# A ninth output tile by quarters in the first feed-forward's second column half, and eight DRAM sums of the second feed-forward made in its own input stage

## The chip, the cores and the metric

The kernel runs on one core of a Trainium2 chip. A core has a matrix engine (PE, with its weight loads shown as PEld), a vector engine (DVE), ScalarE (ACT), GpSimd (POOL) and SyncE (SP), which here only issues DMAs. The engines run their own lists of instructions in order and wait for each other by semaphores. The metric is the device time of one execution in microseconds (us): the median of three runs of the kernel before is 915.06 us (914.81 to 915.23).

## The reference

One decoder layer over 512 tokens of width 1024, in float32:

```python
x = x + 0.5 * rms_norm(swiglu_ffn(rms_norm(x, norm_pre[l, 0]), ffn1_w_in[l], ffn1_w_out[l]), norm_post[l, 0])
mixed = token_mixer(rms_norm(x, norm_pre[l, 1]), w_mix_in[l], ...)
x = x + rms_norm(mixed, norm_post[l, 1])
x = x + 0.5 * rms_norm(swiglu_ffn(rms_norm(x, norm_pre[l, 2]), ffn2_w_in[l], ffn2_w_out[l]), norm_post[l, 2])
```

`swiglu_ffn` multiplies by `w_in` (1024 x 5632), takes `silu(gate) * up` and multiplies by `w_out` (2816 x 1024). The change concerns this last product of the two feed-forwards, 512 x 2816 by 2816 x 1024.

## The kernel before

**Precision.** Each operand is split into a high part (a cast, on ACT) and a low part (the source less the high part, on DVE), and a product is three matmuls: high x high, high x low, low x high. So each weight tile of 128 x 1024 costs one cast on ACT (line 294) and one subtraction on DVE (line 296), and each tile of activations the same (lines 884 and 885).

**Output stage of a feed-forward** (`ffn_out`). The 2816 hidden rows are 11 tiles of 256 rows, numbered 0 to 10 (`k2`). The output's 1024 columns are two halves of 512. For each half the tiles run in the order that `OUT` gives, and each adds into four PSUM banks `C`. A *plain* tile (`plain`, line 1004) takes 48 matmuls of 128 x 256: 4 chunks of 128 tokens, 2 column quarters, 2 row halves, 3 products of parts. A tile that `QUARTERED` names runs *by quarters* (`quartered` and `product`, line 1012): activations and weights are cut in four blocks, and 7 products of sums of blocks, 6 matmuls each, take the place of 8; four more banks `M` collect four of the products. After the last quartered tile of a half `common` combines these on DVE (ACT copies one), and `add` adds the results into `C` (both line 969 for DVE).

In a half's list the last `LAST` tiles, four in the first feed-forward, do not run tile by tile but chunk by chunk (`chunk`): all four for tokens 0 to 127, then all four for the next 128, so that each chunk can be normalised while the next one runs. In the first chunk the four stand one after the other, later the two column quarters do. `add` for the odd chunks stands ahead of them, `add` for the even ones behind the first chunk.

**Where quarters and sums lie.** Quarters of the activations are made once (`h_quarters`): for tiles 2, 4, 6, 8 in parts of the transposed input (`PLACES`), for tile 3 in two of the three buffers called "raw", for tiles 5, 7 and 9 (`APART`) one part in a "raw" buffer and one in the buffer of the gain row ("gpre"). The sums of blocks (`h_sums`) of a tile that runs by quarters in both halves stay in place of the activations themselves (`stay`); the others go to the buffer "xn". Each half splits the sums again into a three-buffer ring "s" (`s_tile`, `s_place`), in which plain tiles lie too. Tile 7's plain activations of the second half lie where the quarters of 4 and 8 were (`LATER`): the high part in 4's place, the low part in 8's.

**Weights.** `ffn_items` and `mix_items` give the list of weight tiles in the order of their use, `weights` works out after which split each may be loaded. Loads go through two rings of raw buffers ("raw", 3, and "raw2", 5), all issued by SP (line 255); split weights lie in four slots (`WBUF`), and a slot comes free when PE has used its tile. Of a quartered tile's own weights three quarters are split (128 x 768); a second item holds the four sums of its blocks.

**Sums in DRAM.** The sums of weight blocks are made in DRAM (`sums_ahead`): three copies on SP's queue (lines 938 to 940, 512 KB), then three DMAs on POOL's queue that add (line 944), each a step of its own. `make_sums` begins one set and moves all begun ones a step. For the first feed-forward it is called in its input stage (`ffn_in`) at every fifth product from number 15, and in the first half of its output stage. For the second, seven sets are copied at the end of the first feed-forward (`copies_early`) and added in the mixer, six are made in the mixer, and two in the first half of its output stage. `behind(x)` orders an instruction behind `x` on its engine, without a semaphore.

**Input stage** (`ffn_in`): a list of products of 24 matmuls each (line 619). DVE adds raw weight tiles to each other there (line 310).

**Order.** A scheduler that works when the program is built gives each engine its list: the earliest in the program among those that are ready by its own model.

Of the kernel before, what the change touches and what calls it, by code (L numbers as in the profile page):

```python
# [23 lines left out]
PAIRS = NF // 2  # L24
# [60 lines left out]


FIRST = (2, 3, 4, 5, 6, 7, 8, 9)
QUARTERED = {"f1": [FIRST, (2, 3, 4, 6, 8)], "f2": [FIRST, (2, 3, 4, 6, 8, 9, 5)]}
OUT = {"f1": [list(range(PAIRS)), [10, 2, 4, 3, 6, 8, 9, 0, 1, 7, 5]]}
OUT["f2"] = [OUT["f1"][0], [10, 2, 4, 3, 6, 8, 9, 5, 7, 0, 1]]  # L90
LAST, APART, TWICE = {"f1": 4, "f2": 2}, (5, 7, 9), (5, 9)
PLACES, LATER = {2: 1, 4: 2, 6: 0, 8: 3}, {7: (2, 3)}

AGAIN, ROWS = (10,), (18, 19, 20, 21)
EVERY, EARLY, AHEAD = 5, 7, 13

# [25 lines left out]
class Layer:  # L124
# [718 lines left out]
    def ffn_in(self):  # L843

        nc = self.nc
        if not self.second:
            self.begun = ()
            self.sums_due("f1")
        for n, (p, t) in enumerate(ORDER2[len(HEADS2) :] if self.second else ORDER[len(HEADS) :]):
            if n > 14 and n % EVERY == 0 and not self.second:  # L850
                self.make_sums()
            if n == 14 and self.second:

                with self.behind(self.pooled):
                    nc.gpsimd.drain()
            with self.behind(*(self.c22 if p in ("p3", "p5") and self.second else ())):
                self.feed()
            self.c22 = []
            self.lag()
            self.prod(p, t)  # L860
            self.after(p, t)
            if t == PAIRS - 1 and p in ("p3", "p7"):
                self.hs.append(self.h_tile(len(self.hs)))
            if n == 1 and not self.second:
                self.lower_bound()
        self.feed()
        self.lag()
# [96 lines left out]
    def ffn_out(self, gpost_row, scale, after, trans, head):  # L964
# [3 lines left out]
        nc, mm = self.nc, self.nc.tensor.matmul  # L968
        tt = lambda out, a, b, op: nc.vector.tensor_tensor(out, a, b, op=op)
        f = "f2" if self.second else "f1"  # L970
        OF, QF, LF = OUT[f], QUARTERED[f], LAST[f]
        low = self.low
        seq = [(half, k2) for half in range(2) for k2 in OF[half]]
        made = deque((h, None) for h in self.hs)
# [1 line left out]
        kept, again = {}, deque()  # L976

        def more(n):
            while count[0] < min(n, len(seq)):
                half, k2 = seq[count[0]]  # L980
                count[0] += 1
                if k2 in QF[half]:
                    if k2 not in kept or half and k2 in TWICE:
                        stay = k2 in QF[1] and k2 not in TWICE
                        a = self.h_quarters(k2, PLACES.get(k2))
                        with self.behind(*([] if stay else [low])):
                            kept[k2] = a, self.h_sums(k2, stay)
                    a, f = kept[k2]
                    made.append((a, self.s_tile(f)))
                elif half and k2 in AGAIN:  # L990
                    made.append(again.popleft())
                else:
                    made.append((self.h_tile(k2, self.x_place(*LATER[k2]) if half and k2 in LATER else None), None))
                    if not half and k2 in AGAIN:
                        again.append(made[-1])
# [58 lines left out]

        with self.behind(*([self.loaded] if self.second else [])):
            g = self.gain("gpost", gpost_row)
        if self.second:
            self.sums_due("f2", done=AHEAD)
        n = 0
        for half in range(2):  # L1060
            C = [[self.ps() for _ in range(2)] for _ in range(2)]
            M, T, left = None, None, len(QF[half])
            for m, k2 in enumerate(OF[half][: PAIRS - LF * half]):
                more(n + 2)
                h, sums = made.popleft()
                if sums:
                    begin = M is None
                    if begin:
                        M = {p: self.ps() for p in ("p1", "p5", "p7", "p6")}

                    quartered(C, M, h, sums, begin, half and OF[1][m : m + 2] == list(TWICE)[::-1])
                    left -= 1
                    if left == 0:
                        T = common(M, [self.hf[:, j, :] for j in ROWS] if half else [self.st("c") for _ in range(4)])
                else:
                    w = self.pull()
                    more(len(seq) if half and m == PAIRS - LF - 1 else n + 3)
                    for i in (0, 2, 1, 3):
                        for v in range(2):
                            plain(C, w, h, i, v, m == 0)  # L1080
                        if i > 1 and T and m == PAIRS - 1:
                            add(C, T, i % 2)
                    self.drop(w)
                n += 1
                if half == 0 and n % 2:
                    self.make_sums()
                if n == 1:
                    self.prod("p4", PAIRS - 1)
                    self.after("p4", PAIRS - 1)
                self.lag()  # L1090
# [687 lines left out]
    def mixer(self):  # L1778
        nc, tc = self.nc, self.tc
        self.got, self.jobs = set(), deque()  # L1780
        self.sums_due("f2", AHEAD, EARLY)
        with tc.tile_pool(name="ma", bufs=1) as ma:
            self.vh = ma.tile([P, NT, NH, P], F32, name="vh")
            self.qk = ma.tile([P, NT, T], F32, name="qk")
# [193 lines left out]
```

## Time and profile before

| | |
|---|---|
| Median of three runs | 915.06 us |
| The profiled execution | 914.82 us |
| its span, first to last instruction | 913.1 us |
| PE busy | 904.7 us |
| DVE busy | 767.1 us |
| ACT busy | 522.3 us |
| matmuls | 7330 |
| first feed-forward, input stage | about 46 to 223 us |
| its output stage | about 223 to 339 us |
| second feed-forward, input stage | about 626 to 795 us |
| its output stage | about 795 to 907 us |

The profile is of one execution. Each row of a timeline gives start, duration, engine, line, operation, output <- inputs, shapes, a count where equal neighbours were merged, and in brackets the engine's idle time before it with what ended it. Rows of waits give the waiting engine with its tile and line, what it waited for, and us in total, times, longest. A busy time counts an engine's instructions; for PE it is modelled, so spacing from start to start is the better measure of its pace.

### The profile page before, as it was taken

How to read it: one execution, taken by the hardware profiler on the slowest of the kernel's cores; microseconds unless marked ns; L12 is line 12 of the kernel's file. 1: busy time of each engine (PE TensorE's matmuls, PEld its weight loads, DVE VectorE, ACT ScalarE, POOL GpSimd, SP SyncE). 2: the span in 40 equal slices, each digit the busy share in tenths (PEclk: the TensorE clock that was granted, in tenths of full speed). 3: DMA queues.
4: the chain of work that ended last, by engine and by line, in shares of the span. 5: the costliest groups of instructions: out<-in, count | busy, mean ns of one | idle time of the engine just before them, and what ended most of it. 6: DMA issues, size and time to landing. Idle time of an engine off the chain costs nothing.

```text
span 913.1 us, 18148 instructions
## 1 busy us (share of the span) xinstructions
PE 904.7 (99%) x7330; PEld 874.7 (96%) x7330; DVE 767.1 (84%) x1005; ACT 522.3 (57%) x749; POOL 183.2 (20%) x256
## 2 busy tenths in 40 slices
PE   9999999999999999999999999999999999999997
PEld 8999999999999999998888888899999999999997
DVE  6899988889888876699986655699899889988886
ACT  7645545557566557857643345694445545757661
POOL 2541112121111047742230300313000000010002
PEclk9999999999999999999999999999999999999999
DMA  9355779775897825899953127053354445388542
GB/s 311 83 161 140 186 191 213 188 156 137 222 273 237 249 62 143 158 200 210 204 119 116 40 76 253 24 162 95 97 156 140 139 130 156 101 238 242 171 144 93
DMA packets 127921, 146.51 MB, mean 160 GB/s; under 512 B 16335, under 2 KB 100303, under 8 KB 127837
## 3 DMA queue, kind: packets, MB, share of 16 engines
q1 hardware_dynamic: 111868, 130.14, 46.8%
q0 software_dynamic: 15680, 14.69, 11.8%
q8 instruction: 57, 0.93, 0.4%
q10 hardware_dynamic: 288, 0.52, 0.2%
q14 instruction: 28, 0.22, 0.1%
HBM read 143.20 MB, written 31.48 MB: 191 GB/s over the span
## 4 chain that ended last, share of the span: by engine, by line
PE 62%; ACT 0%; DVE 0%; DVEq 0%; POOLq 0%; issue 0%; POOL 0%; ACTq 0%
PE ps L619 23%; PE ps L1012 8%; PE ps L549 6%; PE ps L198 5%; PE ps L200 5%; PE ps L199 5%; PE ps L1004 4%; PE ps L560 1%; PE ps L1441 1%; PE ps L364 1%; PE ps L1540 0%; PE ps L1742 0%; PE ps L1491 0%; PE ps L1715 0%; PE ps L1739 0%; PE ps L1505 0%
## 5 line engine op out<-in xcount | busy, mean ns | idle before, releaser
L294 ACT CAST w<-raw 128x1024 fp32r<-128x1024 f32 x246 | 250.9, 1027 | 190.6 <-PE ps L619 91.7
L296 DVE TENSOR_TENSOR w<-raw,w 128x1024 fp32r<-128x1024 f32 x246 | 299.4, 1221 | 30.7 <-ACT w L294 29.5
L619 PE MATMUL ps<-xq,w 128*128 128x256 f32 x2016 | 236.9, 277 | 0.0
L619 PEld LDWEIGHTS ps<-xq,w 128*128 128x128 f32 x2016 | 232.8, 188 | 0.0
L619 PE MATMUL ps<-sq,w 128*128 128x256 f32 x1512 | 177.6, 276 | 0.0
L619 PEld LDWEIGHTS ps<-sq,w 128*128 128x128 f32 x1512 | 174.2, 188 | 0.0
L310 DVE TENSOR_TENSOR raw<-raw,raw 128x1024 f32<-128x1024 f32 x72 | 89.8, 1252 | 7.1 <-DMA raw<-in_ffn_w_in_dram 5.6
L1012 PE MATMUL ps<-w,hs 128*128 128x256 f32 x672 | 80.9, 276 | 0.0
L1004 PE MATMUL ps<-w,hs 128*128 128x256 f32 x672 | 79.2, 276 | 0.0
L1012 PEld LDWEIGHTS ps<-w,hs 128*128 128x128 f32 x672 | 78.3, 188 | 0.0
L1004 PEld LDWEIGHTS ps<-w,hs 128*128 128x128 f32 x672 | 77.5, 188 | 0.0
L198 PE MATMUL ps<-w,xq 128*128 128x512 f32 x176 | 71.1, 404 | 0.0
L200 PE MATMUL ps<-w,xq 128*128 128x512 f32 x176 | 68.9, 392 | 0.0
L199 PE MATMUL ps<-w,xq 128*128 128x512 f32 x176 | 68.6, 390 | 0.0
L944 POOL DMA_DIRECT2D f2sums<-in_ffn_w_out_dram x15 | 20.2, 1522 | 178.6 <-DMA f2sums<-in_ffn_w_out_dram 178.1
L549 PE MATMUL ps<-xq,w 128*128 128x256 f32 x480 | 55.7, 278 | 0.0
L549 PEld LDWEIGHTS ps<-xq,w 128*128 128x128 f32 x480 | 54.9, 188 | 0.5 <-issue 0.5
L884 ACT CAST hs<-hf 128x1024 fp32r<-128x1024 f32 x32 | 33.7, 1053 | 27.4 <-PE ps L1012 19.7
L885 DVE TENSOR_TENSOR hs<-hf,hs 128x1024 fp32r<-128x1024 f32 x32 | 39.1, 1223 | 9.0 <-ACT hs L884 8.4
L944 POOL DMA_DIRECT2D f1sums<-f1sums x26 | 22.0, 847 | 108.6 <-DMA f1sums<-in_ffn_w_out_dram 57.4
L944 POOL DMA_DIRECT2D f2sums<-f2sums x30 | 26.3, 911 | 85.7 <-DMA f2sums<-in_ffn_w_out_dram 44.6
L310 POOL TENSOR_TENSOR raw<-raw,raw 128x1024 f32<-128x1024 f32 x12 | 32.6, 2722 | 40.9 <-DVE w L296 40.7
(263 smaller groups left out, 1234.2 us busy)
## 6 DMA issues: line engine op xcount, KB each, us to landing
raw<-in_ffn_w_in_dram SPq DMA_DIRECT2D x98, 512.0 KB, 4.7
raw<-in_ffn_w_out_dram SPq DMA_DIRECT2D x44, 512.0 KB, 5.5
raw<-in_w_mix_in_dram SPq DMA_DIRECT2D x28, 512.0 KB, 4.7
raw<-f2sums SPq DMA_DIRECT2D x15, 512.0 KB, 5.1
raw<-f1sums SPq DMA_DIRECT2D x13, 512.0 KB, 6.4
raw<-in_w_mix_out_dram SPq DMA_DIRECT2D x8, 512.0 KB, 4.3
f2sums<-in_ffn_w_out_dram SPq DMA_DIRECT2D x30, 128.0 KB, 4.9
f2sums<-in_ffn_w_out_dram SPq DMA_DIRECT2D x15, 256.0 KB, 6.4
```

Source lines behind the costliest of these rows:

```text
L198: mm(ps, sh, mh, start=start, stop=False, **kw)
L199: mm(ps, sh, ml, start=False, stop=False, **kw)
L200: mm(ps, sl, mh, start=False, stop=stop, **kw)
L294: nc.scalar.copy(hi, raw)
L296: self.low = nc.vector.tensor_tensor(lo, raw, hi.bitcast(F32), op=ALU.subtract)
L310: added = (nc.vector if late else nc.gpsimd).tensor_tensor(o, o, c, op=ALU.add)
L549: mm(ps[:, u0:u1], w[:, a, k, :], self.xop(k, b, u0, u1), start=k + n + m == 0, stop=k == ND - 1 and n == 2, skip_group_check=True,)
L619: self.nc.tensor.matmul(ps[:, c], wb[b][:, k, v], left[d][:, k, :], start=first and a + n + k == 0, stop=n == 2 and k == KH - 1, skip_grou ...
L885: self.nc.vector.tensor_tensor(lo, src, hi.bitcast(F32), op=ALU.subtract)
L944: nc.gpsimd.dma_start(to[:, a:b], v, accum_op=ALU.add)
L1004: mm(out, a[kk][:, i * P : (i + 1) * P], w[:, b, kk, QUARTER * v : QUARTER * (v + 1)], start=begin and c == kk == n == 0, stop=kk == 1 and ...
L1012: mm(ps[:, QUARTER * c : QUARTER * (c + 1)], A[a][:, c], B[b], start=begin and c == n == 0, stop=n == 2, skip_group_check=True,)
```

## The change

Tile 9 runs by quarters in the second half of the first feed-forward too, where it was plain, and stands second in the order (10, 9, 2, 4, 3, 6, 8, then 0, 1, 7, 5) where it stood seventh. Its sums and quarters are those of the first half, kept in the "xn", "raw" and gain buffers. `TWICE` becomes a list for each feed-forward, empty for the first. The sums of the first feed-forward are 14 sets instead of 13, and the calls of `make_sums` in the input stages begin at product 10. The second feed-forward makes eight sets (all but the seven early ones) in its own input stage; the mixer only finishes the early ones.

```diff
-QUARTERED = {"f1": [FIRST, (2, 3, 4, 6, 8)], "f2": [FIRST, (2, 3, 4, 6, 8, 9, 5)]}
-OUT = {"f1": [list(range(PAIRS)), [10, 2, 4, 3, 6, 8, 9, 0, 1, 7, 5]]}
+QUARTERED = {"f1": [FIRST, (2, 3, 4, 6, 8, 9)], "f2": [FIRST, (2, 3, 4, 6, 8, 9, 5)]}
+OUT = {"f1": [list(range(PAIRS)), [10, 9, 2, 4, 3, 6, 8, 0, 1, 7, 5]]}
-LAST, APART, TWICE = {"f1": 4, "f2": 2}, (5, 7, 9), (5, 9)
+LAST, APART, TWICE = {"f1": 4, "f2": 2}, (5, 7, 9), {"f1": (), "f2": (5, 9)}
...
-EVERY, EARLY, AHEAD = 5, 7, 13
+EVERY, EARLY = 5, 7
...
-            self.sums_due("f1")
+        self.sums_due(*(("f2", None, EARLY) if self.second else ("f1",)))
...
-            if n > 14 and n % EVERY == 0 and not self.second:
+            if n > 9 and n % EVERY == 0:
                 self.make_sums()
...
-        OF, QF, LF = OUT[f], QUARTERED[f], LAST[f]
+        OF, QF, LF, two = OUT[f], QUARTERED[f], LAST[f], TWICE[f]
...
-                    if k2 not in kept or half and k2 in TWICE:
-                        stay = k2 in QF[1] and k2 not in TWICE
+                    if k2 not in kept or half and k2 in two:
+                        stay = k2 in QF[1] and k2 not in APART
...
-        if self.second:
-            self.sums_due("f2", done=AHEAD)
...
-                    quartered(C, M, h, sums, begin, half and OF[1][m : m + 2] == list(TWICE)[::-1])
+                    quartered(C, M, h, sums, begin, half and OF[1][m : m + 2] == list(two)[::-1])
...
-        self.sums_due("f2", AHEAD, EARLY)
+        self.sums_due("f2", EARLY, EARLY)
```

## The prediction

> **What bounds the kernel now.** I read the page's head first, then the waits of the matrix engine (PE) alone, then the chain of work that ended last, in order of time.
>
> ```profile
> span 913.1 us, 18148 instructions
> PE 904.7 (99%) x7330; PEld 874.7 (96%) x7330; DVE 767.1 (84%) x1005; ACT 522.3 (57%) x749; POOL 183.2 (20%) x256
> PE ps L194 <- POOL ones L172: 1.2, 1, 1.2
> PE ps L364 <- DVE xn L754: 0.5, 1, 0.5
> PE ps L619 <- ACT xq L384: 0.2, 1, 0.2
> 595.65 199.00 PE ps L619 x1752
> 794.65 5.44 PE ps L1004 x48
> 808.25 38.08 PE ps L1012 x336
> ```
>
> PE waits for others 1.9 us in all, three times, by the three rows of its waits. In the chain its matmuls follow each other without a gap: 48 plain ones (L1004) take 5.44 us, 336 of the quartered kind (L1012) 38.08 us, which is 113.3 ns each in both, and 1752 of the input stage (L619) 199.00 us, 113.6 ns each. So the time is the number of matmuls, and nothing that is taken from the vector engine (DVE), from ScalarE (ACT) or from a DMA can be gained. Only two things move the end: fewer matmuls, or a new wait of PE.
>
> **The ninth tile by quarters.** A plain output tile is 48 matmuls (4 token chunks, 2 column quarters, 2 row halves, 3 products of high and low parts), a quartered one 42 (7 products of 2 x 3). Six go: 6 x 113.3 ns = **-0.68 us**, all on the path. The Trainium skill ("TensorE: Matmul & The Clock Gate", section "Wait — 56ns, not 53.3ns?") gives the spacing of warm matmuls as columns over 2.4 GHz plus some 2.5 ns; for 256 columns that is an estimate of 109 ns, and the six would be worth 0.66 us by it. The rows say 113.3 ns and decide.
>
> For the six matmuls the change adds one more set of sums of tile 9: three copies on SP's queue, three adding DMAs on POOL's, one more load of 512 KB, one more split of 1024 columns, while the split of tile 9's own weights shrinks from 1024 to 768. The activations cost no new DVE work: quarters and sums of tile 9 exist since the first half, and their second split stands where the plain tile's split stood. Beside five quartered tiles of the same kind, all without a PE wait, I cost these at nothing. The hiding is the 4.76 us that PE needs for a tile.
>
> **Buffers held longer.** Tile 9's quarters lie in a "raw" buffer and in the gain buffer, and stay there now until its second use. Before, both came free with its first use:
>
> ```profile
> 275.12 0.42 SPq L255 DMA_DIRECT2D raw<-in_w_mix_in_dram  x1
> 275.59 2.67 SPq L165 DMA_DIRECT2D gpre<-in_norm_pre_dram  x1
> 300.08 1.29 SPq L255 DMA_DIRECT2D raw<-in_w_mix_in_dram  x2
> 326.48 1.43 DVE L481 SCALAR_TENSOR_TENSOR xn<-xs,col,gpre 128x512 f32<-128x512 f32 x2 [2.06 <-POOL col L458]
> ```
>
> The first mixer weight and the gain row are loaded at 275. As tile 9 is now the second of the half, they can be issued one plain and one quartered tile later, about 290, and the two loads at 300 (tile 3's buffers) one tile later, about 305. The gain row is read first at 326, so some 30 us of cover are left. Cost nothing. SP loses 2.67 us to the gain row at the new place instead of the old one; loads behind it have the five-buffer ring as cover.
>
> **The end of the half.** Here the change takes a cushion away. Before, the order was 8 (quartered), 9 (plain), then the last four tiles 0, 1, 7, 5 chunk by chunk. Under the 5.44 us of plain tile 9, DVE combined the products of the quarters (L969), split the last activations (L885) and the last weights (L296). Now tile 8 is directly followed by the four.
>
> ```profile
> 306.12 2.88 PE L1012 MATMUL ps<-w,hs 128*128 128x256 f32 x24
> 308.85 0.84 PE L1012 MATMUL ps<-w,xq 128*128 128x256 f32 x6
> 309.52 8.32 PE L1004 MATMUL ps<-w,hs 128*128 128x256 f32 x72
> 308.09 1.23 DVE L296 TENSOR_TENSOR w<-raw,w 128x1024 fp32r<-128x1024 f32 x1 [0.35 <-ACT w L294]
> 309.23 0.68 DVE L969 TENSOR_TENSOR hf<-ps,hf 128x512 f32<-128x512 f32 x1
> 309.83 1.22 DVE L885 TENSOR_TENSOR xq<-hf,xq 128x1024 fp32r<-128x1024 f32 x1
> 310.96 0.69 DVE L969 TENSOR_TENSOR hf<-ps,hf 128x512 f32<-128x512 f32 x1
> 311.56 1.22 DVE L296 TENSOR_TENSOR w<-raw,w 128x1024 fp32r<-128x1024 f32 x1
> 312.69 0.68 DVE L969 TENSOR_TENSOR hf<-hf,ps 128x512 f32<-128x512 f32 x1
> 313.29 1.22 DVE L885 TENSOR_TENSOR hs<-hf,hs 128x1024 fp32r<-128x1024 f32 x1
> 314.43 0.69 DVE L969 TENSOR_TENSOR hf<-ps,hf 128x512 f32<-128x512 f32 x1
> 315.03 1.29 DVE L969 TENSOR_TENSOR ps<-ps,hf 128x512 f32<-128x512 f32 x2
> 316.25 1.23 DVE L885 TENSOR_TENSOR hs<-hf,hs 128x1024 fp32r<-128x1024 f32 x1
> 317.40 1.22 DVE L296 TENSOR_TENSOR w<-raw,w 128x1024 fp32r<-128x1024 f32 x1
> 309.05 1.06 ACT L884 CAST hs<-hf 128x1024 fp32r<-128x1024 f32 x1 [0.99 <-PE ps L1012]
> ```
>
> Tile 8 ends on PE at 309.52; plain tile 9 would end at 314.96. DVE is busy without a hole from 308.09 to 318.6: weights (tile 1's next in the ring), then the four combining steps with the splits between them, the two additions, and last the activations and weights of tile 5. Start to start a split takes 1.14 us and a combining step or an addition 0.61.
>
> After the change tile 8 ends one quartered tile later, 309.52 + 4.76 = 314.28, and the four tiles begin at once, 12 matmuls or 1.36 us each in the first chunk: 0 at 314.28, 1 at 315.64, 7 at 317.00, 5 at 318.36; the second chunk at 319.72. What needs tile 8's end cannot move forward: the low part of tile 7 (it overwrites tile 8's quarters), the activations of tile 5 (buffer of tile 8's sums; ACT began that kind of cast at 309.05, so 313.81 now), the weights of tile 5 (slot of tile 8's sums), and the combining. Tile 1's activations are done before, one tile's distance earlier than in these rows.
>
> DVE's list by the order of the rows, shifted by 4.76: weights of 7 from 312.85, combining 1 to 314.60, low part of 7 to 315.73, combining 2 to 316.34, weights of 5 to 317.48, combining 3 to 318.09, activations of 5 to 319.23, combining 4 to 319.84, addition for column quarter 0 to 320.45. PE wants tile 7's low part at 317.2 (there is cover of 1.5 us), tile 5's weights at 318.47 (1 us), tile 5's low activations, its third matmul, at 318.59: it gets them at about 319.3, **0.7 us late**. The first chunk then ends at 320.4 and the addition comes 0.1 us late. Sum: +0.76 us. If DVE takes the third and fourth combining step behind everything PE waits for, the lateness is 0.1; if it takes both before tile 5's activations and starts with combining instead of weights, 1.6. I take 0.76, because the rows show one split between each two combining steps, and keep both ends. Queued behind the late split are the fourth step and the additions; the next chunk and the output of chunk 0 wait for them, nothing else does.
>
> **The eight sums of the second feed-forward.** Six leave the mixer and two leave the output stage; all eight go to the input stage, calls at products 10 to 60. PE waits nowhere in the mixer, so nothing is won there. What they meet is this:
>
> ```profile
> DMA to landing us min/median/max: 3.7/5.6/9.8
> DMA to landing us min/median/max: 3.5/3.6/4.6
> DVE raw L310 <- DMA raw<-in_ffn_w_in_dram: 5.6, 3, 2.1
> 664.78 25.48 SPq L255 DMA_DIRECT2D raw<-in_ffn_w_in_dram  x8
> 679.63 1.23 DVE L310 TENSOR_TENSOR raw<-raw,raw 128x1024 f32<-128x1024 f32 x1 [1.54 <-DMA raw<-in_ffn_w_in_dram]
> 686.25 1.22 DVE L296 TENSOR_TENSOR w<-raw,w 128x1024 fp32r<-128x1024 f32 x1
> 804.09 1.25 POOL L944 DMA_DIRECT2D f2sums<-in_ffn_w_out_dram  x1 [174.79 <-DMA f2sums<-in_ffn_w_out_dram]
> 128.90 0.60 SPq L940 DMA_DIRECT2D f1sums<-in_ffn_w_out_dram  x1
> ```
>
> The first two rows are the "raw" tile's in two windows: loads land after 5.6 us (median) in the first feed-forward's input stage, 60 to 185 us, where sums are made, and after 3.6 in the second's, 640 to 785, where none are. In the second, DVE waits for a load three times already, 2.1 us at most. POOL's queue is free there (idle 175 us up to 804). The Trainium skill ("DMA: Bandwidth & Descriptors", section "Issuing engines are not separate DMA queues") says that DMAs of all issuers run on the same 16 engines and interleave; the two medians agree, and it is the rule that speaks against this part.
>
> The worst place is 679.63. The second and third sum are both ordered behind the last load of tile 4, so six copies of 0.60 us of SP time each stand ahead of tile 5's loads. PE's product 24 of this stage begins, 38 products of 2.73 us before 794.65, at 691.0 and reads low parts 0.9 us later; DVE had that split done at 686.25 + 1.22 = 687.5: 4.4 us of cover. With the median of the first stage a load is 2.0 us later, and PE sees nothing. With its longest (9.8 against 4.6) it is 5.2 later, and PE stands 0.8 us. I cost it at 0.
>
> The first feed-forward's calls begin at product 10 instead of 15, but both calls are ordered behind the same load (the last of tile 4), so the 14 sums end where the 13 did. Nothing.
>
> **Sum.** 914.82 us (the profiled execution's own time; 1.7 us lie around its span) - 0.68 + 0.76 = 914.9. The median of the runs shown is 0.24 above that execution, so 915.1 for the measured one: the change gives back at the end of the half what it saves in it.
>
> **Rivals.** *The six matmuls stay saved* (0.30): DVE does the splits first, wait 0.1, 914.5 on the median. For it: the same slots, and an order that is set ahead of time could put the split first. Against it: in the rows the combining steps never wait for a split that is ready beside them by more than one. *Late weight loads in the second input stage* (0.12): the same mechanism at all the tiles' bursts, each over the cover by 0.8 us or, where two sums stand ahead of one burst, by 2. It decides when a load lands more than 4.4 us later than now. Two such places and the forecast's wait give 915.1 + 1.5 to 4, about 917: slower. Against it: with sums in the first stage DVE has no DMA among its waits at all. *The order of DVE or SP elsewhere changes* (0.06), by up to 2 us either way. The forecast itself has 0.52; between 0.1 and 1.6 us of wait it is 914.5 to 916.0.
>
> **Chances.** A measurement of this kernel can tell about 0.2% (1.8 us) from no change, so all cases but the late loads are "the same": same 0.86, slower 0.10 (most of the late loads, some of the reordering), faster 0.04 (reordering alone, since six matmuls are a third of what counts). The range goes from the saved case less 0.4 of scatter (914.1) to the lower late loads (916.5).
>
> **What would show it.** L1012 has 42 more matmuls and L1004 48 fewer. Tile 8's last matmul comes directly before the four tiles. PE's waits gain one row with L1004 and DVE as releaser, or a gap in L1004's spacing some 4 us after tile 8, of 0.7 us; no gap there means the first rival. Loads of the second input stage land at 5 to 6 us in the median, and DVE's wait for them grows above 5.6 us; a PE wait at L619 means the second. A change of more than 2 us with none of these would make my reading wrong altogether.

## The result and the profile after

| | before | after |
|---|---|---|
| median of the timed runs | 914.93 us (914.67 to 915.23, 4 runs) | 926.44 us (924.40 to 928.48, 4 runs) |
| ratio, 95% interval | | 1.0127 (1.0106 to 1.0148) |
| profiled execution, its own time | 914.82 us | 928.48 us |
| its span | 913.1 us | 926.6 us |

The changed kernel is slower by 11.5 us, far above the predicted range. One run of a kernel further down took 1531 us at a granted clock of 0.56 where its others took 915 to 922, and is left out of its median. Of the prediction's rivals one came about, the late weight loads in the second input stage, at two to six times its price: 8.7 us by the run of that part alone, where it was given 1.5 to 4. The head of the page after, two of its groups of instructions and its row of weight loads (its last figure is the median from issue to landing, 4.7 before):

```profile
span 926.6 us, 18156 instructions
PE 908.3 (98%) x7324; PEld 877.2 (95%) x7324; DVE 765.3 (83%) x1006; ACT 522.6 (56%) x750; POOL 187.6 (20%) x259
L310 DVE TENSOR_TENSOR raw<-raw,raw 128x1024 f32<-128x1024 f32 x72 | 89.7, 1250 | 20.0 <-DMA raw<-in_ffn_w_in_dram 18.6
L1004 PE MATMUL ps<-w,hs 128*128 128x256 f32 x624 | 74.0, 277 | 0.3 <-DVE hs L885 0.3
raw<-in_ffn_w_in_dram SPq DMA_DIRECT2D x98, 512.0 KB, 5.1
```

PE has its six matmuls fewer (x7324 against x7330), and L1004 has 48 fewer (672 before). But DVE stood 18.6 us at L310, the addition of two raw weight tiles, until a weight load had landed; before it was 5.6 us. Of the waits of PE alone, after, those that bear on the change (total, times, longest, in us):

```profile
PE ps L619 <- DVE ps L638: 7.1, 3, 4.7
PE ps L619 <- DVE w L296: 1.6, 1, 1.6
PE ps L560 <- ACT w L294: 0.7, 1, 0.7
PE ps L1004 <- DVE hs L885: 0.3, 1, 0.3
```

The first two rows are new: 8.7 us at L619 in the second input stage, most of it for L638, of which the prediction said nothing. The timeline of the place, first PE, then DVE (start, duration, then in brackets the idle time ahead and what ended it):

```profile
687.03 1.98 PE L619 MATMUL ps<-xq,w 128*128 128x256 f32 x16
690.56 3.91 PE L619 MATMUL ps<-xq,w 128*128 128x256 f32 x32 [1.55 <-DVE w L296]
699.13 4.58 PE L619 MATMUL ps<-sq,w 128*128 128x256 f32 x24 [4.66 <-DVE ps L638]
...
678.96 0.68 DVE L638 TENSOR_TENSOR hf<-ps,hf 128x512 f32<-128x512 f32 x1
688.14 1.23 DVE L310 TENSOR_TENSOR raw<-raw,raw 128x1024 f32<-128x1024 f32 x1 [8.50 <-DMA raw<-in_ffn_w_in_dram]
...
698.29 0.69 DVE L638 TENSOR_TENSOR ps<-ps,hf 128x512 f32<-128x512 f32 x1
```

And the same two instructions before, from its timeline, for tile 4 and for tile 6:

```profile
689.78 0.69 DVE L638 TENSOR_TENSOR ps<-ps,hf 128x512 f32<-128x512 f32 x1
738.55 0.69 DVE L638 TENSOR_TENSOR ps<-ps,hf 128x512 f32<-128x512 f32 x1
...
691.02 2.88 PE L619 MATMUL ps<-sq,w 128*128 128x256 f32 x24
740.04 2.88 PE L619 MATMUL ps<-sq,w 128*128 128x256 f32 x24
```

L638 at 689.78 is the subtraction that the function `after` issues for product p5 of tile 4: the bank of p5 less a copy, written into the bank on which product p6 then adds. It ended at 690.47, and p6 began at 691.02: 0.55 us of cover, the time by which it can be late before PE waits. For tile 6 it is 740.04 - 739.24 = 0.80. DVE works its list in order, so whatever makes DVE late, a load ahead of an addition too, makes this subtraction late. After, DVE stood 8.50 us for the load, was busy without a hole from then on (before, it was busy for 132.9 of the 145 us from 640 to 785, or 92%, which leaves little to catch up with), and p6 began at 699.13. The wait of 1.55 us ahead of it is that for the late load's own data: before, their low part was split at 682.0, and PE, whose third set of eight matmuls in a product reads it, wanted it at 685.58 + 1.82 = 687.4, so they had 5.4 us of cover.

The same row shows the second price: 24 matmuls took 4.58 us instead of 2.88. The windows, after first and then before (the numbers are busy us and instructions of PE, PEld, DVE, ACT, POOL, then the granted clock of PE, the DMA share and GB/s):

```profile
699.40:702.80 3.40, 3.40 (x18) 3.40 (x17) 3.37 (x5) 0.64 (x2) 0.85 (x1) 0.50 0.90 188
752.00:786.00 34.00, 34.00 (x289) 34.00 (x290) 29.60 (x32) 15.89 (x20) 4.51 (x5) 1.00 0.79 197
```

```profile
699.40:702.80 3.40, 3.40 (x32) 3.40 (x31) 3.31 (x4) 1.71 (x3) 0.00 (x0) 1.00 0.46 148
752.00:786.00 34.00, 34.00 (x302) 34.00 (x302) 31.88 (x39) 19.37 (x27) 0.00 (x0) 1.00 0.47 140
```

Behind the wait of 4.66 us the granted clock was 0.50 for 3.41 us, which costs half of it, 1.7 us. And in the 34 us from 752, behind a wait of 1.99 us at tile 6's p6, PE ran 289 matmuls instead of 302 at a granted clock of 1.00: 13 x 0.1133 = 1.5 us, of which more below. At the end of the first feed-forward the trace loses 0.44 us in the first chunk and 0.66 us more than before at the mixer's first product, and wins 0.68. So of the 13.66 us between the two profiled executions, 8.7 are the waits, 1.7 the half clock, 1.5 the slower matmuls, 0.4 the end of the first feed-forward; 0.3 lie in the start of the kernel (the first L619 at 11.40 instead of 11.07), where the change does nothing, and some 1.1 us I do not place.

### The profile page after: what moved, and what is told of

It is laid out like the page before. It is cut to its first block, busy times and chain, and to the rows that moved or that the text cites. A ratio compares the mean times of both kernels' runs of the same rounds, so it can differ in the third digit from the quotient of the medians.

```text
span 926.6 us, 18156 instructions
## 1 busy us (share of the span) xinstructions
PE 908.3 (98%) x7324; PEld 877.2 (95%) x7324; DVE 765.3 (83%) x1006; ACT 522.6 (56%) x750; POOL 187.6 (20%) x259
## 4 chain that ended last, share of the span: by engine, by line
PE 50%; DVE 5%; DMA 3%; issue 3%; POOL 1%; ACT 1%; DVEq 0%; POOLq 0%; ACTq 0%
PE ps L619 12%; PE ps L1012 8%; PE ps L549 6%; PE ps L198 5%; PE ps L200 5%; PE ps L199 5%; PE ps L1004 4%; DMA raw<-in_ffn_w_in_dram 3%; DVE w L296 3%; DVE raw L310 1%; PE ps L560 1%; PE ps L1439 1%; POOL raw L310 1%; PE ps L364 1%; DVE ps L638 1%
## 5 line engine op out<-in xcount | busy, mean ns | idle before, releaser
L294 ACT CAST w<-raw 128x1024 fp32r<-128x1024 f32 (+1 forms) x247 | 251.4, 1026 | 201.2 <-PE ps L619 79.6
L296 DVE TENSOR_TENSOR w<-raw,w 128x1024 fp32r<-128x1024 f32 (+1 forms) x247 | 300.2, 1219 | 32.3 <-ACT w L294 30.9
L619 PE MATMUL ps<-xq,w 128*128 128x256 f32 x2016 | 237.6, 277 | 1.6 <-DVE w L296 1.6
L619 PEld LDWEIGHTS ps<-xq,w 128*128 128x128 f32 x2016 | 233.3, 188 | 1.8 <-DVE w L296 1.8
L619 PE MATMUL ps<-sq,w 128*128 128x256 f32 x1512 | 180.2, 278 | 7.1 <-DVE ps L638 7.1
L619 PEld LDWEIGHTS ps<-sq,w 128*128 128x128 f32 x1512 | 176.5, 189 | 7.6 <-issue 7.0
L310 DVE TENSOR_TENSOR raw<-raw,raw 128x1024 f32<-128x1024 f32 x72 | 89.7, 1250 | 20.0 <-DMA raw<-in_ffn_w_in_dram 18.6
L1012 PE MATMUL ps<-w,hs 128*128 128x256 f32 x696 | 83.7, 276 | 0.0
L1012 PEld LDWEIGHTS ps<-w,hs 128*128 128x128 f32 x696 | 81.1, 188 | 0.0
L1004 PE MATMUL ps<-w,hs 128*128 128x256 f32 x624 | 74.0, 277 | 0.3 <-DVE hs L885 0.3
L1004 PEld LDWEIGHTS ps<-w,hs 128*128 128x128 f32 x624 | 72.1, 188 | 0.5 <-DVE hs L885 0.5
L944 POOL DMA_DIRECT2D f1sums<-f1sums x28 | 24.0, 857 | 117.3 <-DMA f1sums<-in_ffn_w_out_dram 55.8
L310 POOL TENSOR_TENSOR raw<-raw,raw 128x1024 f32<-128x1024 f32 x12 | 32.6, 2723 | 40.9 <-DVE w L296 40.7
L200 PEld LDWEIGHTS ps<-w,xq 128*128 128x128 f32 x176 | 33.0, 188 | 7.5 <-DVE xq L371 0.3
```

The source lines that it names most:

```text
L200: mm(ps, sl, mh, start=False, stop=stop, **kw)
L294: nc.scalar.copy(hi, raw)
L296: self.low = nc.vector.tensor_tensor(lo, raw, hi.bitcast(F32), op=ALU.subtract)
L310: added = (nc.vector if late else nc.gpsimd).tensor_tensor(o, o, c, op=ALU.add)
L619: self.nc.tensor.matmul(ps[:, c], wb[b][:, k, v], left[d][:, k, :], start=first and a + n + k == 0, stop=n == 2 and k == KH - 1, skip_grou ...
L944: nc.gpsimd.dma_start(to[:, a:b], v, accum_op=ALU.add)
```

## The experiments

The theory after the result, A: the copies of the moved sums stand ahead of the weight loads in SP's queue and share the DMA engines with them; the loads land late, DVE waits, and PE waits for L638. The rivals are in the expectations, where the letters B and C can stand for other things from run to run. Each run is compared with runs of the kernel before on the same chip (medians 914.74 to 915.16 us).

**The two parts apart.** The first part alone: of the change, the edits to the second feed-forward's sums are undone.

```diff
...
-        self.sums_due(*(("f2", None, EARLY) if self.second else ("f1",)))
+        if not self.second:
+            self.sums_due("f1")
...
-            if n > 9 and n % EVERY == 0:
+            if n > 9 and n % EVERY == 0 and not self.second:
...
+        if self.second:
+            self.sums_due("f2", done=AHEAD)
...
-        self.sums_due("f2", EARLY, EARLY)
+        self.sums_due("f2", AHEAD, EARLY)
```

> The first feed-forward's part alone; the second feed-forward makes its sums where the kernel before does (six in the mixer, two in the output stage). Theory A (the loss is the DRAM copies that stand ahead of weight loads in the second input stage): about 915.4 us, that is -0.68 for six matmuls, +0.43 for the wait at tile 5's activations and some +0.6 where the mixer's first product waits for the late chain of the chunks, and no wait of PE after 345 us. Rival C (the first part shifts the order of everything behind it): several us above 915, with waits in the second input stage.

The second part alone is the change without its edits to QUARTERED, OUT, TWICE and the places that read them; the calls for the first feed-forward's sums begin at product 15, as before.

> The eight sums of the second feed-forward in its input stage, on the kernel before. Theory A: about 924 to 927 us, with the same waits of PE for DVE near product 22 to 24 (together above 5 us). Rival C: about 915.

The first part alone: 916.99 us (915.80 to 922.58, 10 runs), 1.0033 (1.0015 to 1.0051), no PE wait in the second input stage. The second alone: 923.62 us (921.95 to 924.67, 4 runs), 1.0093 (1.0076 to 1.0110), and the waits of the change:

```profile
PE ps L619 <- DVE ps L638: 5.1, 2, 4.7
```

So the second part is most of the loss, some 8.7 of 11.5 us; rival C, that the first part shifts everything behind it, falls. The first part costs 2.0 us, more than predicted and more than the 915.4 us expected for it here, and its runs scatter by 7 us; that is taken up at the end.

**One set at a time.** The two sets that are begun at one call (the prediction's worst place) are spread.

```diff
-                self.make_sums()
+                self.make_sums(not (self.second and n == 20))
...
-    def make_sums(self):
+    def make_sums(self, begin=True):
...
-        if n < 2 and self.ahead:
+        if begin and n < 2 and self.ahead:
```

> The whole change, but the call at product 20 of the second input stage begins no set, so that one set of copies, not two, stands behind the last load of tile 4, and each later set comes one call later. Theory A (two sets of copies, 1 MB in SP's queue ahead of tile 5's loads): the load that landed after 11.9 us lands in 5 to 7, the waits of 1.6 and 4.7 us go with the throttled stretch behind them, and the time is 917 to 919. Rival B (any traffic of the sums in this stage, POOL's adding DMAs above all): above 922 us, with the waits only moved.

924.09 us (918.76 to 927.62, 5 runs), 1.0090 (1.0060 to 1.0121): theory A is missed, and it is what rival B forecast, above 922 with the waits only moved. The wait at tile 4 is gone, but one has come up at tile 6 (timeline of PE):

```profile
744.90 5.46 PE L619 MATMUL ps<-sq,w 128*128 128x256 f32 x24 [3.44 <-DVE ps L638]
```

Tile 6's p6 has 0.80 us of cover before. Single sets make loads late enough to use that up; the pair was not the point.

**Copies and adding DMAs apart.** One kernel issues the copies of the eight sets in the mixer and leaves the adding DMAs where the change has them.

```diff
...
-            self.making.append(self.sums_ahead(*self.ahead.popleft()))
+            g = self.sums_ahead(*self.ahead.popleft())
+            if self.park:
+                next(g)
+                self.parked.append(g)
+            else:
+                self.making.append(g)
+        elif not self.park and self.parked:
+            self.making.append(self.parked.popleft())
...
```

> The whole change, but the three copies of each of the eight sets are issued in the mixer; only POOL's adding DMAs stay in the second input stage. Theory A: no wait of PE there, 915.0 to 916.5 us. Rival B (POOL's adding DMAs delay the loads): above 920 us.

940.88 us (938.25 to 943.51, 4 runs), and it tells something else. As nothing held them in the second input stage, the adding DMAs were issued in the mixer too, in POOL's queue ahead of POOL's selects (`affine_select`), for which DVE waits and then PE:

```profile
PE ps L1680 <- DVE pT L1642: 20.9, 1, 20.9
```

The second input stage, without any DMA of the sums, had no PE wait in this run. Two more kernels separate them, both on the second part alone: one leaves out the 24 adding DMAs, and with them the additions of these sums; one has the copies in the mixer and each adding DMA held in the stage by a one-column copy on POOL.

```diff
...
-                nc.gpsimd.dma_start(to[:, a:b], v, accum_op=ALU.add)
+                f == "f2" and self.second or nc.gpsimd.dma_start(to[:, a:b], v, accum_op=ALU.add)
...
```

> The second part of the change alone, with the 24 adding DMAs of its eight sets left out (the second half's sums of the second feed-forward are then copies, not sums); the 24 copies on SP's queue stay where they are. Theory A (the copies stand ahead of the weight loads in SP's queue and share the DMA engines with them): loads land late as with the adds, PE waits for DVE's subtraction (L638) at some product p6 by 2 us or more, 919 to 924 us. Rival B (the adding DMAs of POOL's queue slow the loads): no PE wait in the stage, 915 to 916. Rival C (it is the sum of both kinds of traffic; either alone stays nearly under the cover): loads late by 1 to 3 us, PE waits under 1 us, 915 to 917.

```diff
...
-            with self.behind(*([self.selected] if f == "f2" else [])):
+            seen = [nc.gpsimd.tensor_copy(self.col(), self.half(self.whole[0], 0)[:, 0, :1])] if self.second else []
+            with self.behind(*([self.selected] if f == "f2" else []), *seen):
...
```

> The counterpart: the copies of the eight sets are issued in the mixer, and only their 24 adding DMAs stay in the second input stage, each behind a one-column copy on POOL that reads an activation of the tile finished last, so that none can be issued in the mixer. Theory A: no PE wait in the stage, 915 to 916. Rival B: PE waits at L638 by 2 us or more, 919 to 924. Rival C: as for the copies alone, 915 to 917.

Copies alone: 918.10 us (917.36 to 918.14, 5 runs), 1.0034 (1.0022 to 1.0047). Adding DMAs alone: 917.21 us (915.56 to 923.52, 10 runs), 1.0039 (1.0022 to 1.0056). The first row of PE's waits in each, copies first:

```profile
PE ps L619 <- DVE ps L638: 1.6, 1, 1.6
```

```profile
PE ps L619 <- DVE ps L638: 3.5, 2, 3.1
```

By the medians neither A nor B: the rival that it is the sum of both is nearest, though both lie above its 915 to 917. Each kind of traffic alone costs about 2.5 to 3.4 us, both together 8.7. By the medians that is more than the sum; by the intervals (2.0 to 4.3, 2.0 to 5.1 and 7.0 to 10.1 us) the sum is not excluded. The profiled executions say this with two limits. That of the copies took 918.10, as the median, but of its 3.2 us over the kernel before only 2.6 arise in this stage; 1.1 lie in a stretch of slower matmuls from 47 us on, ahead of any of these copies. That of the adding DMAs took 923.52, the slowest of the ten runs: by its wait of 3.1 us and the half clock behind it rival B's sign is there in this run, but the median run cannot have lost as much. The weight loads of the stage, issue to landing, as far as the traces tell their landing (8 to 20 of some 34), in us: 3.5/3.6/4.6 before (least, median, most), 3.4/4.6/8.4 with the copies, 3.6/5.3/8.9 with the adding DMAs, and after the change

```profile
DMA to landing us min/median/max: 3.6/4.9/11.8
```

For the load that DVE stood for in the changed kernel, two rows of SP tell whether it was issued late or landed late, after first and then the same load before:

```profile
676.20 0.37 SPq L255 DMA_DIRECT2D raw<-in_ffn_w_in_dram  x1
```

```profile
674.65 0.37 SPq L255 DMA_DIRECT2D raw<-in_ffn_w_in_dram  x1
```

PE was 1.45 us behind the kernel before at that place (687.03 against 685.58), so the load was issued 0.1 us late; it is the one of 11.8 us and landed about 7 us late. So SP's time for issuing the six copies is not what made this load late; it lost its time between issue and landing. That adding DMAs suffice for late loads, with no copy ahead in SP's queue, the run with them alone shows. How much the copies add by standing ahead in the queue and how much by using the same DMA engines is not told apart.

**The cover itself.** In the kernel before, without any sums in the stage, DVE's subtraction for p5 is done four times for tile 4 (cover 0.55 us) and for tile 7 (5.99 us), with PE's order pinned.

```diff
...
-            tt(self.two_by(q), self.two_by(bank["p5", t]), h1, ALU.subtract)
+            [tt(self.two_by(q), self.two_by(bank["p5", t]), h1, ALU.subtract) for _ in range(4 if self.second and t in (4, 7) else 1)]
```

> The kernel before, with no sums in the second input stage, but DVE's subtraction between the products p5 and p6 done four times instead of once (same operands, same result) for tile 4 and for tile 7 of that stage, and PE's order pinned to that of before. Three more at 0.61 us from start to start are 1.8 us. Theory: the cover of a late DVE is the one at p6: 0.55 us for tile 4, 5.99 for tile 7. PE waits 1.3 us for L638 at tile 4's p6, not at all at tile 7's, and the time is 916.1 to 916.5. Rival (the prediction's cover, 4.4 us by the low parts of the weights): no PE wait at all, 914.8 to 915.2.

919.10 us (916.63 to 920.53, 5 runs), 1.0045 (1.0032 to 1.0058). In the timelines, tile 4 first, then tile 7 (L620 is L619 there):

```profile
692.25 2.62 DVE L638 TENSOR_TENSOR ps<-ps,hf 128x512 f32<-128x512 f32 x4
695.02 4.26 PE L620 MATMUL ps<-sq,w 128*128 128x256 f32 x24 [3.10 <-ACT ps L653]
...
757.91 0.70 DVE L638 TENSOR_TENSOR ps<-ps,hf 128x512 f32<-128x512 f32 x1
759.35 2.88 PE L620 MATMUL ps<-sq,w 128*128 128x256 f32 x24
```

Tile 4's last repeat ends at 694.87, and PE starts 0.15 us behind it, the distance it has behind L638 in the changed kernel too; the row names ACT's L653, which ended in the same moment, but p6 does not need that: before, it began at 692.24, when p6 was under way. The subtraction is done 4.4 us later than before (690.47), 3.7 if one takes off that PE itself was 0.7 us behind there. That is more than the 1.8 I gave it, because a weight split and another subtraction were placed between the repeats. PE waits 3.10 us, about the 3.7 less 0.55 of cover. At tile 7 the last repeat ends at 758.61, 11.0 us later than the one subtraction before (747.64), of which 5.7 are PE's own shift (759.35 against 753.64); of 5.99 us of cover 0.74 are left, and PE does not wait. The theory holds in place and kind; the size was off, and behind the 3.10 us stands a half clock of 3.41 us that I had not reckoned with. Wait and half clock, 3.10 + 1.7 us, are most of the 5.7 that this profiled execution, the slowest of the five, lost.

**More cover for tile 4.** On the second part alone, product p2 of tile 4 goes ahead of p6.

```diff
+for _t in (4,):
+    _n = ORDER2.index(("p6", _t))
+    ORDER2[_n : _n + 2] = ORDER2[_n + 1], ORDER2[_n]
```

> The second part of the change alone (the eight sums in the second input stage, as in the run of that part, 923.62 us), with one edit: of tile 4, product p2 goes ahead of p6, so that DVE's subtraction between p5 and p6 has one product, 2.72 us, more of cover there (0.55 + 2.72 = 3.3 us). Theory: the loads land as late as in that run, but PE's wait for L638 at tile 4's p6 falls from 4.7 to about 2, under the 3.1 us behind which the clock was halved, so that the half clock (6.83 us at half, 3.4 us) goes too: 923.6 - 2.7 - 3.4 = 917.5, within 916 to 919.5. Rival (the late loads themselves are the bound, through the weights that are split from them): PE waits as long for the weights (L296) instead, 922 or more.

921.92 us (920.75 to 923.20, 4 runs), 1.0073 (1.0060 to 1.0086): only 1.7 us better, outside the 916 to 919.5 expected.

```profile
695.66 2.98 PE L619 MATMUL ps<-sq,w 128*128 128x256 f32 x24 [1.66 <-DVE ps L638]
...
746.43 4.60 PE L619 MATMUL ps<-sq,w 128*128 128x256 f32 x24 [3.28 <-DVE ps L638]
```

At tile 4 the wait fell to 1.66 us and the half clock behind it went, as the theory had it; PE did not wait longer for weights, so the rival falls. But now tile 6, whose cover was left at 0.8, waited 3.28 us with a half clock behind it. With several thin places and loads late by chance, one place mended is not the stage mended.

**The first part: the cushion.** Two ways to put 5.44 us of plain matmuls back between tile 8 and the chunks: three tiles by chunks instead of four, or plain tile 10 moved there.

```diff
-LAST, APART, TWICE = {"f1": 4, "f2": 2}, (5, 7, 9), {"f1": (), "f2": (5, 9)}
+LAST, APART, TWICE = {"f1": 3, "f2": 2}, (5, 7, 9), {"f1": (), "f2": (5, 9)}
```

> The first part of the change alone, with the last three tiles of the first feed-forward chunk by chunk instead of the last four, so that tile 0 stands as a plain tile (48 matmuls, 5.44 us) between the quartered tile 8 and the chunks, as tile 9 did before. If the missing 5.44 us of plain matmuls are what cost 0.44 us in the first chunk and 0.66 at the mixer's start, both gaps go and the six matmuls are won: 914.2 to 914.6. Rival (the chunks, now of 18 matmuls per column quarter instead of 24, are too short for DVE's work between them): new PE waits in the chunks, 915.5 or more.

```diff
...
-OUT = {"f1": [list(range(PAIRS)), [10, 9, 2, 4, 3, 6, 8, 0, 1, 7, 5]]}
+OUT = {"f1": [list(range(PAIRS)), [9, 2, 4, 3, 6, 8, 10, 0, 1, 7, 5]]}
...
-AGAIN, ROWS = (10,), (18, 19, 20, 21)
+AGAIN, ROWS = {"f1": (), "f2": (10,)}, (18, 19, 20, 21)
...
```

> The first part of the change alone, with plain tile 10 moved from the front of the second half to the place between the quartered tile 8 and the last four (order 9, 2, 4, 3, 6, 8, 10, then 0, 1, 7, 5), so that 5.44 us of plain matmuls lie there as tile 9's did before; its activations are split a second time for it (before, the split of the first half was used again), and a bank is opened by the first product into it. If the missing cushion is what the first part costs: no PE wait for L886 in the first chunk and the mixer's start as before, 914.96 - 0.68 = 914.3, within 914.0 to 914.9. Rival (something else of the ninth quartered tile costs it): 916 to 917 as with the first part alone.

Three tiles: 920.13 us (918.71 to 923.25, 5 runs), 1.0054 (1.0041 to 1.0068); the rival. PE waits for the normalised rows of the chunks, which the shorter chunks do not cover:

```profile
PE ps L364 <- DVE xn L481: 1.5, 2, 1.2
...
PE ps L364 <- DVE hf L481: 1.1, 1, 1.1
```

These are 2.6 us of the 8.4 that this profiled execution, at 923.25 the slowest of the five, is behind the kernel before. In the mixer PE waits 1.7 us more (L1442), and matmuls ran slower at full clock in stretches between 346 and 419 us; the loss is not fully taken apart.

Tile 10 moved: the waits at the chunks are gone (one of 0.4 us for L491 comes up at the front of the half), but the median is 918.37 us, 1.0038 (1.0022 to 1.0054), with runs from 915.19 to 922.16. Two further profiles of it were to show where the long runs lose their time.

> The kernel of the run with tile 10 ahead of the last four, once more: its twelve times lay between 915.19 and 922.16 us, while the profiled one (916.42) had no PE wait in the second input stage. Theory: the longer ones have the same stall as the eight sums bring, PE waiting for DVE's subtraction (L638) ahead of a product p6 with 0.2 to 0.8 us of cover, because one weight load landed late by chance. If this profile is one above 918 us, it shows such a wait and, where the wait is above 3 us, the half clock. Rival: the time is lost at many places or at the start, with no wait above 1 us.

> As the run before it, for a second profile of the same kernel: theory and rival as there.

The first took 914.87 us, the second 920.49 us, beside 915.16 for the kernel before. Neither waited in the second input stage; the theory falls. The long one stood in the mixer (waits of PE, then timelines of POOL and DVE):

```profile
PE ps L1677 <- DVE pT L1639: 4.1, 1, 4.1
...
486.17 0.81 POOL L945 DMA_DIRECT2D f2sums<-f2sums  x1 [2.73 <-DMA f2sums<-f2sums]
486.76 1.50 POOL L1629 TENSOR_SCALAR_AFFINE_SELECT e<-e 128x512 f32<-128x512 f32 x2
487.72 1.29 DVE L1639 SCALAR_TENSOR_TENSOR pT<-ps,e 128x512 f32<-128x512 f32 x2 [9.80 <-POOL e L1629]
```

The same instructions in the kernel before:

```profile
472.56 0.81 POOL L944 DMA_DIRECT2D f2sums<-f2sums  x1 [2.82 <-DMA f2sums<-f2sums]
473.16 1.51 POOL L1624 TENSOR_SCALAR_AFFINE_SELECT e<-e 128x512 f32<-128x512 f32 x2
...
481.89 1.28 DVE L1634 SCALAR_TENSOR_TENSOR pT<-ps,e 128x512 f32<-128x512 f32 x2
```

POOL issues the adding DMAs of the mixer one behind the other, each behind the landing of what it reads, and the selects stand behind the last. Before, the last issue of that chain began at 472.56 and the first pair of selects ended at 474.67, 7 us ahead of DVE's need. In the first part alone the last issue began at 479.65, and in this run at 486.17. The last two runs take one of the 13 sets out of the mixer (the output stage makes it), with the orders of PE, DVE and ACT unchanged:

```diff
-EVERY, EARLY, AHEAD = 5, 7, 13
+EVERY, EARLY, AHEAD = 5, 7, 12
```

> The first part alone with tile 10 moved ahead of the last four, and one set of the second feed-forward's sums made in the output stage instead of the mixer (12 sets there instead of 13); orders of PE, DVE and ACT are the same as without. Theory (POOL's chain of adding DMAs in the mixer made the scatter): the selects come some 9 us sooner, about 474, DVE does not wait for them over 1 us, no run above 917, median 914.5 to 915.0. Rival (the scatter has another source): runs up to 922 again, median above 916.5. Rival 2 (the set is now late in the output stage, where the DMA engines are over 90% busy): PE waits there, 915.5 or more.

> The first part as the change has it (tile 8 directly ahead of the last four), with 12 sets in the mixer instead of 13. Theory: without the scatter of the mixer what is left is the lost cushion: -0.68 for the six matmuls, +0.44 in the first chunk, +0.66 - 0.24 at the mixer's start, so 914.96 + 0.2 = 915.2, within 914.9 to 915.9, no run above 917.5. Rival: 916.5 and above as before, with long runs.

With tile 10 moved: 915.84 us (914.67 to 917.93, 11 runs), 1.0013 (1.0004 to 1.0022). As the change has it: 916.14 us (915.39 to 917.29, 11 runs), 1.0014 (1.0005 to 1.0024). The long runs are gone, and in the profile of the first the selects begin long before DVE needs them, and DVE waits for PE alone:

```profile
464.42 0.65 POOL L1629 TENSOR_SCALAR_AFFINE_SELECT e<-e 128x512 f32<-128x512 f32 x1 [2.85 <-ACT e L1628]
479.35 1.29 DVE L1639 SCALAR_TENSOR_TENSOR pT<-ps,e 128x512 f32<-128x512 f32 x2 [0.32 <-PE ps L1637]
```

So POOL's chain made the scatter, by one long run that was profiled and by the two kernels in which a shorter chain took it away; why the chain runs later in the kernels with the first part than before is not shown. Both medians are above what I expected, by about 1 us, and one run, 917.93, is above the 917 set for the first; no version tried beats the kernel before. The first part costs 2.0 us as the change has it and about 1.3 without the scatter, not the 0.1 that was predicted. The two gaps and the six matmuls explain 0.4 of it; putting the cushion back by tile 10 took the gaps away and gained only 0.3, within the intervals, so the rest is open.

## Why the prediction was wrong

*Six matmuls, -0.68.* Right: x7324, with 48 of L1004 gone.

*The end of the half, +0.76 for tile 5's activations.* Right in place and kind, less in size, and incomplete. The wait in the chunk and the mixer's first product after, on PE's timeline, with the post-processing of chunk 0 on DVE's:

```profile
319.84 2.88 PE L1004 MATMUL ps<-w,hs 128*128 128x256 f32 x23 [0.27 <-DVE hs L885]
339.72 5.48 PE L560 MATMUL ps<-xq,w 128*128 128x256 f32 x46 [0.74 <-ACT w L294]
...
322.19 0.42 DVE L501 TENSOR_TENSOR hf<-ps,gpost 128x256 f32<-128x256 f32 x1
```

The step from matmul to matmul is 0.44 us longer than usual at 319.29, where 0.76 was predicted. But the prediction said that only the next chunk and the output of chunk 0 wait for what is queued behind the split. The post-processing of chunk 0 is queued there; it began 0.96 us later than before (321.23; 0.3 of it from the kernel's start), each chunk's behind it, and the mixer's first product waited 0.74 us for a weight cast that ACT has queued behind this output. Of the measured 1.27 us these two gaps and the six matmuls give 0.4.

*The eight sums at 0.* This is the step that failed: "DVE had that split done at 686.25 + 1.22 = 687.5: 4.4 us of cover". Three things were wrong in it, and the runs show each. (The 4.4 itself is a slip too: the low part is read after 16 matmuls, 1.8 us into the product and not 0.9, which makes it 5.3.) The cover was taken from weight data alone (the low part that product 24 reads), while DVE, in order, holds up everything behind the waiting addition; the first thing behind it that PE needs is L638, with 0.55 us, and the four-fold subtraction showed that this cover, not the 4.4, is what counts. The load was later than the longest of the first input stage, 11.8 us against 9.8: beside the 4.6 of before it is 7.2 late where I allowed 5.2. And a wait of PE was priced as itself, while the waits above 3 us here brought half a clock with them. The first two make the forecast's condition for the rival ("more than 4.4 us later than now") wrong; by the cover of 0.55 to 0.80 us at tiles 4 and 6 it decides with nearly any delay, and its chance of 0.12 was far too small.

The page of the Trainium skill that the prediction named against this part holds as far as it goes: DMAs of all issuers share the 16 engines ("DMA: Bandwidth & Descriptors", section "Issuing engines are not separate DMA queues"). With the adding DMAs on POOL's queue alone, none of them ahead of a load in SP's, the loads' median rose from 3.6 to 5.3 us.

*Nothing is won in the mixer.* PE does not wait there before, so this is right for that kernel. But the runs of the first part show what the sets do there: POOL's chain ends 7 us ahead of need in one kernel and behind it in another that differs only in the first feed-forward. The change takes this hazard away and pays for it in the stage behind.

*What would show it.* The sign of the second rival, "a PE wait at L619 means the second", came as it was named. The loads' median in that stage, forecast at 5 to 6 us for that case, came to 4.9; it was the longest, not the median, that decided.

## What to carry to other kernels

The cover of a late transfer is not that of its own data: go through the in-order engine's list behind the instruction that waits for it, and take the smallest distance to a need of the bound engine. DVE, 92% busy here, did not catch up, so its delay travelled until it met the thinnest place. And price a wait of PE in steps: up to 2 us it cost itself here, above 3 us the clock as well, and no wait between was measured.

## What the runs showed of the hardware

*The clock behind a wait.* Behind PE waits of 3.10 us (the four-fold subtraction), 3.28, 4.07 and 4.66 us the granted clock was 0.50 for 3.41 us, with 3.1 (the adding DMAs alone), 3.44 and 4.7 us for 6.83, with one of 20.9 us for 20.48; behind 1.55, 1.66 and 1.99 it stayed at 1. The longer stretches began while PE still waited, so that less of them was run through: 4.8 to 6.1 of the 6.83 us and 4.6 of the 20.48 lay behind the wait, and half of that is the price. Stretches at full clock are whole multiples of 3.41 us as well (the 692.91 us ahead of the half clock in the changed kernel are 203 of them), so the clock changed on a fixed grid. In the step ahead of each half clock PE stood 2.0 to 3.4 us (2.0 in the four-fold subtraction, 693.01 to 695.02 in a step that ends at 696.42); steps at full clock in which it stood at most 1.7 us were not followed by one (1.66 at tile 4 with more cover, 694.00 to 695.66). The window of the four-fold subtraction:

```profile
696.40:699.80 3.40, 3.40 (x19) 3.40 (x18) 1.04 (x3) 1.53 (x2) 0.00 (x0) 0.50 0.55 158
```

The Trainium skill ("TensorE: Matmul & The Clock Gate", section "Part 1: The HAM clock gate") tells of a free-running window of some 3.4 us and half the clock behind an idle one; the lengths, one, two and six times 3.41, agree, and the wait of 3.10 us shows that one shorter than the window can do.

*Slower matmuls at full clock.* In some profiles matmuls of 256 columns followed each other 117.8 ns apart instead of 113.3, for 10 to 48 us, at a granted clock of 1.00, and then went back. It mostly began at a break in PE's sequence, of 0.06 us or of 2, sometimes at none that the trace shows, and most breaks were not followed by it. In the first part with 12 sets it began at tile 6's p6, where L638 ended 0.17 us ahead, and cost 10 matmuls, 1.1 us, beside the kernel before:

```profile
740.00:772.00 32.00, 32.00 (x274) 32.00 (x273) 27.93 (x30) 15.21 (x20) 0.00 (x0) 1.00 0.48 150
```

```profile
740.00:772.00 32.00, 32.00 (x284) 32.00 (x284) 28.51 (x31) 15.66 (x20) 0.00 (x0) 1.00 0.53 155
```

This accounts for most of what that profile lost beyond the two gaps of the first part. What sets it off was not tried, and it stays open.
